# Gated linear attention: gate projection ahead of the values, Silu applied later in place

## The chip, the cores and the metric

The kernel runs on one core of one Trainium2 chip. The metric is the device time of one execution in microseconds (us). Three runs of the kernel before took 2588.95, 2592.64 and 2594.71 us, so the median is 2592.64 us. One further execution was profiled; all rows below come from it.

## The reference

A two-layer decoder trunk over 1024 tokens of width 1024, in float32. Layer 0 mixes tokens by differential attention, layer 1 by gated linear attention (GLA); each is followed by a gated MLP with a short convolution. The change touches only GLA, which has 4 heads with keys of 128 and values of 256:

```
q, k, v, r = split(h @ w_in)                      # per head: 128, 128, 256, 256 columns
g = log_sigmoid((h @ w_a1) @ w_a2 + b_a) / 16
b = cumsum(g) inside a chunk
attn[i,j] = sum_d q[i,d] k[j,d] exp(b[i,d] - b[j,d]),  j <= i
o = (q exp(b)) @ state + attn @ v
state = exp(b_last) state + (k exp(b_last - b))^T @ v
out = (rms_norm(o) * silu(r)) @ w_o
```

## The kernel before

Every large product is made from a high and a low part of each operand (hi*hi, hi*lo, lo*hi), so a weight block of 128x1024 is loaded by DMA into a staging buffer `st` (three of them), its high part is cast on ScalarE (line 122, `wh`) and its low part is taken on GpSimd (line 123, `wl`). There are two `wh` and two `wl` buffers. `load_w` hands out blocks in the order of the list `order` and has the next one split ahead as far as a buffer is free.

A head's projections are cut into units. `qk_units` has 4 (queries and keys, two token halves each), `r_units` 4 (the output gate r, two halves of 128 columns by two token halves), `v_units` 8 (values, one for each block of 128 tokens). A q, k or r unit is 24 matmuls with 512 columns and ends in one 128x512 eviction from PSUM; a v unit is 24 matmuls with 256 columns and ends in a ScalarE cast and a VectorE subtraction. A v unit needs both of the head's value blocks, so v holds both weight buffers until its last unit; q, k and r need one block for two units. Units are closures; `run(units, n)` takes the next n of a list at the place in the program where it stands. A scheduler then fixes one instruction order for each engine, in which work that is not ready gives way to later work that is; on the chip each engine runs its order as it stands.

One head goes through these stages in the loop over `hd`:

- `decay(hd)`: b from the gate's low-rank input `z1`: a matmul `psg`, Abs, Exp and Ln on ScalarE, a GpSimd subtraction, eight scans on VectorE.
- levels: attention inside chunks of 128 is built from a diagonal and 7 levels. `prepare(m)` makes one scaled operand `d` (two VectorE subtractions, one ScalarE Exp, one GpSimd product with k, one VectorE product with q), `put` multiplies it with itself on TensorE into `psl` (two PSUM buffers) and copies the valid part into `acc` on VectorE (lines 996 and 998). `d` comes from a ring of four buffers.
- `across`, `inside`, `cross`, `key_T`: q and k scaled for use across chunks, `acc` split into parts, the products between neighbouring chunks (`psx`), the transposed keys (`psk`).
- `state`: three steps of the running state (`pss`); `outputs` and `finish`, for two token halves (`og`): output, norm, product with silu(r) (line 1087), and later (`rest`, lines 274 to 286 and 1097) the scale by the norm, written to DRAM (for the last head, kept in SBUF).

Before, the 8 value units of a head begin at the end of the head before it (2 units) and go on in its levels; the 4 r units stand at `inside`, `cross` and `state`, and are evicted by Silu straight from PSUM (line 913). After the last of them an instruction (line 916) loads ScalarE's table with Exp and Ln back. The 4 q and k units of the next head follow at `state` and `outputs`. After the last head the list ends with the units of the output projection (`first_units`, tile `pacc`).

Of the kernel before, what the change touches and what calls it, by code (L numbers as in the profile page):

```python
# [13 lines left out]
AF = mybir.ActivationFunctionType  # L14
# [7 lines left out]
NT = T // P  # L22
# [24 lines left out]
def trunk(ctx, tc, x, norm_mix, norm_ffn, norm_final, wqk, wv, w_o, lam_in, subln,  # L47
          gqk, gv, gr, ga1, ga2, gba, gnorm, g_o, wup, conv, wdn,
          cos_t, sin_t, causal, lvl_mask, ident_in, out):
    nc = tc.nc  # L50
# [27 lines left out]
    def slot(i, name, dt=F32, shape=None):  # L78

        return slots.tile(shape or [P, 1024], dt, name=name, tag=f"s{i}")  # L80
# [23 lines left out]
    order, loaded = [], []  # L104
# [56 lines left out]
    def half(hf):  # L161
        return slice(512 * hf, 512 * hf + 512)
# [684 lines left out]
    def gla(proj):  # L847
# [18 lines left out]
        q, k, b, vs, sr, fac = {}, {}, {}, {}, {}, {}  # L866
# [21 lines left out]
        def qk_units(hd):  # L888
            q[hd], k[hd] = slot(2 * (hd % 2), "q"), slot(2 * (hd % 2) + 1, "k")
            W = {}  # L890

            def unit(s, hf):
                if hf == 0:
                    W[s] = load_w(gqk[2 * hd + s])
                ps = mm_ps("psq")
                project_T(ps, W[s], hf)
                if s == 0:
                    nc.scalar.mul(q[hd][:, half(hf)], ps, DK ** -0.5)
                else:
                    nc.scalar.copy(k[hd][:, half(hf)], ps)  # L900
                flush()
            return [lambda s=s, hf=hf: unit(s, hf) for s in range(2) for hf in range(2)]

        def r_units(hd):
            sr[hd] = [slot(6 + e, "r") for e in range(2)]
            W = {}

            def unit(e, hf):
                if hf == 0:
                    W[e] = load_w(gr[2 * hd + e])  # L910
                ps = mm_ps("psr")
                project_T(ps, W[e], hf)
                last = nc.scalar.activation(sr[hd][e][:, half(hf)], ps, AF.Silu)
                if e == 1 and hf == 1:
                    with tc.issue_after(getattr(last, "ins", last)):
                        nc.scalar.preload_act_table_set("natural_log_exp_and_others")
            return [lambda e=e, hf=hf: unit(e, hf) for e in range(2) for hf in range(2)]

        def v_units(hd):
            vs[hd] = [[slot(14 + 2 * i + hf, "v" + "hl"[i], F32R, [P, 4, DV]) for hf in range(2)] for i in range(2)]  # L920
            W = []

            def unit(t):
                if t == 0:
                    W.extend(load_w(gv[2 * hd + i]) for i in range(2))
                ps = mm_ps("psv")
                project_tok(ps[:, :DV], W, t)
                vh, vl = (z[t // 4][:, t % 4, :] for z in vs[hd])
                nc.scalar.copy(vh, ps[:, :DV])
                nc.vector.tensor_tensor(vl, ps[:, :DV], f32(vh), op=ALU.subtract)  # L930
            return [lambda t=t: unit(t) for t in range(NT)]
# [70 lines left out]
        def across(hd):  # L1002

            bv = b[hd].rearrange("p (c w) -> p c w", c=NCH)
            tot = bv[:, :, CH - 1:CH]
            fac[hd] = small.tile([P, NCH, 1], F32, name="fac", tag="fac", bufs=2)
            nc.scalar.activation(fac[hd], tot, AF.Exp, scale=1.0 / 16)
            kd, qd = d_ring("kd"), d_ring("qd")
            kv = kd.rearrange("p (c w) -> p c w", c=NCH)
            nc.vector.tensor_tensor(kv, tot.broadcast_to([P, NCH, CH]), bv, op=ALU.subtract)  # L1010
            nc.scalar.activation(kd, kd, AF.Exp, scale=1.0 / 16)
            nc.scalar.activation(qd, b[hd], AF.Exp, scale=1.0 / 16)
            nc.gpsimd.tensor_tensor(k[hd], kd, k[hd], op=ALU.mult)
            nc.vector.tensor_tensor(q[hd], qd, q[hd], op=ALU.mult)


        def inside(hd, av):
            EH, EL = (slot(18 + i, "e" + "hl"[i], F32R, [P, 4, 2, P]) for i in range(2))
            O = slot(20, "odd", F32R, [P, 2, 4, P])
            for src, hi, lo in ((av[:, 0::2, :], EH[:, :, 0, :], EL[:, :, 0, :]),  # L1020
                                (av[:, 1::2, :], O[:, 0], O[:, 1])):
                nc.scalar.copy(hi, src)
                nc.gpsimd.tensor_tensor(lo, src, f32(hi), op=ALU.subtract)
            return EH, EL, O

        def cross(hd, A):
            EH, EL, _ = A
            ps = mm_ps("psx")
# [74 lines left out]
        def run(units, n=1):  # L1103
            for _ in range(n):
                if units:
                    units.pop(0)()
# [1 line left out]
        for u in qk_units(0):  # L1108
            u()
        nc.scalar.preload_act_table_set("natural_log_exp_and_others")  # L1110
        nxt = v_units(0)
        gates()
        run(nxt, 2)
        decay(0)
        for hd in range(GH):
            vu = nxt
            av, diagonal, prepare, put = level_units(hd)
            diagonal()
            ds = []
            for n, m in enumerate(LEVELS):  # L1120
                ds.append(prepare(m))
                if n >= 1:
                    put(n - 1, ds[n - 1])
                run(vu)
            put(len(LEVELS) - 1, ds[-1])
            run(vu, NT)
            last = hd == GH - 1
            nxt = r_units(hd) + (proj.first_units() if last else qk_units(hd + 1))
            across(hd)
            A = inside(hd, av)  # L1130
            run(nxt)
            cross(hd, A)
            run(nxt)
            kT = key_T(hd)
            S = slot(21, "S", F32, [P, 3, DV])
            for B in range(3):
                if B < 2:
                    run(nxt)
                state(hd, B, kT, S)
            if not last:  # L1140
                decay(hd + 1)
            run(nxt, 2)
            rest = finish(hd, 0, outputs(hd, 0, A, S))
            run(nxt, 2)
            rest()
            rest = finish(hd, 1, outputs(hd, 1, A, S))
            run(nxt, 1)
            if not last:
                nxt = v_units(hd + 1)
                run(nxt, 2)  # L1150
            else:
                run(nxt, 3)
            rest()
            if last:
                run(nxt, NT)
# [4 lines left out]
    for layer, w_out in enumerate((w_o, g_o)):  # L1160
        order += [w_out[k] for k in ((0, 1, 2, 3, 6, 7), (0, 1, 4, 6, 7))[layer]] + [None]
        if layer == 0:
            order += [gqk[0], gqk[1]]
            for hd in range(GH):
                order += [gv[2 * hd], gv[2 * hd + 1]]
                order += [gr[2 * hd], gr[2 * hd + 1]]
                order += [gqk[2 * hd + 2], gqk[2 * hd + 3]] if hd + 1 < GH else []

    st = {}
# [27 lines left out]
    proj = OutProjection(0, w_o, 0, lambda t: x[t * P:(t + 1) * P, :])  # L1197
# [109 lines left out]
```

## Time and profile before

| | |
|---|---|
| runs | 2588.95, 2592.64, 2594.71 us |
| profiled execution | 2591.02 us, of it 2589.2 us span |
| granted TensorE clock, mean | 0.98 |
| TensorE busy | 2472.1 us (95%) |
| VectorE, ScalarE, GpSimd busy | 63%, 40%, 46% |

The span is the time from the first to the last instruction of the program in the trace; 1.8 us lie around it. PE is TensorE, DVE VectorE, ACT ScalarE, POOL GpSimd, SP the queue that issues DMAs. Rows give the start of an instruction in us from the span's start, its duration, its engine and line, and in brackets how long the engine had been idle before it and what ended that. Matmuls overlap, so the duration of one is longer than the distance to the next. GLA lies between about 1344 and 1800 us of the span.

### The profile page before, as it was taken

To read this page: it belongs to the slowest core of one execution; us is meant where nothing else is said; L and a number is where in the kernel's file an instruction comes from. 1 tells how busy PE (TensorE), PEld (TensorE's weight loads), DVE (VectorE), ACT (ScalarE), POOL (GpSimd) and SP (SyncE) were. 2 spreads that over 40 slices of the span, in tenths; PEclk is the share of its full clock that TensorE was granted. 3 is DMA by queue.
4 is the path that set the end of the run, shared out by engine and by line. 5 is a ranking of instruction groups with operands and counts; after the bars stand their busy time and mean duration, and the time that the engine had idled before them with its cause. 6 is when DMAs were issued, how large, how long until landed. Compare 5 with 4: busy or idle time off the path is not lost. (4 is left out here: it accounts for less than half of the span.)

```text
span 2589.2 us, 30822 instructions
## 1 busy us (share of the span) xinstructions
PE 2472.1 (95%) x11752; PEld 2012.3 (78%) x11752; DVE 1627.7 (63%) x2218; ACT 1032.8 (40%) x1630; POOL 1202.9 (46%) x723
## 2 busy tenths in 40 slices
PE   7999999988999999999998999998889999999998
PEld 5777777776788888788887888787768888887887
DVE  5577777876666666644456467386566666665445
ACT  4454454534454454421133334332245445442111
POOL 3444445325555555554414344353355555554441
PEclk9999999999999999999999999999989999999999
DMA  5222222433122222443221111123312222234331
GB/s 175 64 63 58 58 58 57 126 122 127 63 89 81 75 82 85 176 132 98 93 83 33 50 33 33 50 95 129 110 66 81 88 76 82 84 126 156 114 98 65
DMA packets 66020, 228.61 MB, mean 88 GB/s; under 512 B 8144, under 2 KB 8784, under 8 KB 65872
## 3 DMA queue, kind: packets, MB, share of 16 engines
q1 hardware_dynamic: 65872, 226.64, 26.6%
q8 instruction: 92, 1.51, 0.3%
q14 instruction: 56, 0.46, 0.1%
HBM read 163.17 MB, written 50.86 MB: 83 GB/s over the span
## 5 line engine op out<-in xcount | busy, mean ns | idle before, releaser
L308 DVE TENSOR_TENSOR res<-pacc,res 128x512 f32<-128x512 f32 x408 | 280.0, 690 | 273.4 <-PE pacc L144 272.8
L478 POOL TENSOR_TENSOR uw<-st,uw 128x512 fp32r<-128x512 f32 x190 | 287.9, 1515 | 238.1 <-ACT uw L477 228.4
L123 POOL TENSOR_TENSOR wl<-st,wh 128x1024 fp32r<-128x1024 f32 x55 | 141.5, 2577 | 264.7 <-ACT wh L122 264.7
L142 PE MATMUL pacc<-wdh,gh 128*128 128x512 f32 x512 | 200.7, 394 | 5.9 <-DVE res L308 5.9
L143 PE MATMUL pacc<-wdl,gh 128*128 128x512 f32 x512 | 202.5, 395 | 0.1
L144 PE MATMUL pacc<-wdh,gl 128*128 128x512 f32 x512 | 201.9, 394 | 0.0
L557 DVE SCALAR_TENSOR_TENSOR b<-cu,cv,b 128x1023 f32<-128x1023 f32 x44 | 62.3, 1416 | 186.7 <-ACT b L556 186.7
L477 ACT CAST uw<-st 128x512 fp32r<-128x512 f32 x190 | 118.1, 621 | 110.7 <-PE ps_z L144 55.6
L142 PE MATMUL psq<-XH,wh 128*128 128x512 f32 x384 | 157.2, 410 | 1.2 <-DVE ms L172 0.7
L604 POOL TENSOR_TENSOR gl<-st,gh 128x1024 fp32r<-128x1024 f32 x32 | 78.1, 2439 | 165.1 <-ACT gh L603 122.4
L143 PE MATMUL psq<-XL,wh 128*128 128x512 f32 x384 | 154.2, 401 | 0.5 <-DVE ms L172 0.4
L144 PE MATMUL psq<-XH,wl 128*128 128x512 f32 x384 | 153.1, 399 | 0.0
L753 ACT ACTIVATE p<-p,nmax 128x256 f32<-128x256 f32 (+7 forms) x128 | 99.0, 776 | 86.1 <-DVE nmax L750 84.9
L122 ACT CAST wh<-st 128x1024 fp32r<-128x1024 f32 x59 | 61.6, 1047 | 161.0 <-PE pacc L144 53.3
L142 PE MATMUL pacc<-wh,gh 128*128 128x512 f32 x256 | 107.0, 421 | 19.6 <-DVE XL L239 10.9
L603 ACT CAST gh<-st 128x1024 fp32r<-128x1024 f32 x32 | 33.6, 1049 | 215.5 <-PE pacc L143 157.7
L478 POOL TENSOR_TENSOR wh<-st,wh 128x512 fp32r<-128x512 f32 x56 | 85.6, 1529 | 70.9 <-ACT wh L477 70.9
L142 PEld LDWEIGHTS pacc<-wdh,gh 128*128 128x128 f32 x512 | 96.9, 189 | 27.8 <-DVE res L308 6.7
L478 POOL TENSOR_TENSOR wl<-st,wl 128x512 fp32r<-128x512 f32 x56 | 84.5, 1509 | 66.8 <-ACT wl L477 64.7
L143 PEld LDWEIGHTS pacc<-wdl,gh 128*128 128x128 f32 x512 | 96.9, 189 | 22.9 <-POOL wdl L604 1.0
L144 PEld LDWEIGHTS pacc<-wdh,gl 128*128 128x128 f32 x512 | 96.9, 189 | 21.1
L750 DVE CUSTOM_DVE_ANT_0 p<-s_ps,mask 128x256 f32<-128x256 f32 (+7 forms) x128 | 91.5, 750 | 26.7 <-PE pta L773 22.7
(356 smaller groups left out, 7429.7 us busy)
## 6 DMA issues: line engine op xcount, KB each, us to landing
st<-in_wup_dram SPq DMA_DIRECT2D x88, 512.0 KB, 3.5
g_scr<-a SPq DMA_DIRECT2D x44, 512.0 KB, 2.6
st<-in_wdn_dram SPq DMA_DIRECT2D x44, 512.0 KB, 3.6
st<-g_scr SPq DMA_DIRECT2D x44, 512.0 KB, 3.3
r_scr<-res SPq DMA_DIRECT2D x24, 512.0 KB, 3.2
res<-r_scr SPq DMA_DIRECT2D x24, 512.0 KB, 5.6
st<-in_wqk_dram SPq DMA_DIRECT2D x16, 512.0 KB, 3.5
st<-o_scr SPq DMA_DIRECT2D x13, 512.0 KB, 3.4
```

What stands on the lines that cost most here:

```text
L122: nc.scalar.copy(hi, st)
L123: (eng_lo or nc.gpsimd).tensor_tensor(lo, st, f32(hi), op=ALU.subtract)
L142: nc.tensor.matmul(ps, lhsT=ah, rhs=bh, start=first, stop=False, **kw)
L143: nc.tensor.matmul(ps, lhsT=ah, rhs=bl, start=False, stop=False, **kw)
L144: nc.tensor.matmul(ps, lhsT=al, rhs=bh, start=False, stop=last, **kw)
L308: nc.vector.tensor_tensor(res[t][:, half(dh)], ps, res[t][:, half(dh)], op=ALU.add)
L477: nc.scalar.copy(w[:, half(0)], src)
L478: nc.gpsimd.tensor_tensor(w[:, half(1)], src, f32(w[:, half(0)]), op=ALU.subtract)
L557: nc.vector.scalar_tensor_tensor(u[:, 1:], c[:, :T - 1], cv[:, n, 1:2], u[:, 1:], op0=ALU.mult, op1=ALU.add)
L604: nc.gpsimd.tensor_tensor(lo, st, f32(hi), op=ALU.subtract)
L750: nc.vector.tensor_tensor_reduce(out=pm[:, :w], in0=s_ps[:, :w], in1=st["mask"][:, T - w:], scale=-0.125, scalar=3.0e38, op0=ALU.add, op1= ...
L753: nc.scalar.activation(pm[:, :w], pm[:, :w], AF.Exp, bias=nmax, scale=-1.0, accum_out=sums[:, m:m + 1])
```

## The change

The four r units go ahead of the eight v units in one list. The list is begun at the end of the head before, after `outputs` (2 units; in head 0 after `gates`), goes on in the levels (7 units) and ends at `inside`, `cross` and `key_T` (one unit each). The q and k units of the next head then have a list of their own and begin in `state`. The weight order is changed to match. The r units are evicted by a plain copy; `silu` then applies Silu in place, 128x1024 twice, and is put behind the last Exp of `across` on ScalarE, with the table load behind it. Heads take turns in two pairs of r buffers (slots 26, 27 and 6, 7), since r of the next head is made while the last one's is in use.

```diff
         def r_units(hd):
-            sr[hd] = [slot(6 + e, "r") for e in range(2)]
+            sr[hd] = [slot((26 if hd % 2 == 0 else 6) + e, "r") for e in range(2)]
...
-                last = nc.scalar.activation(sr[hd][e][:, half(hf)], ps, AF.Silu)
-                if e == 1 and hf == 1:
-                    with tc.issue_after(getattr(last, "ins", last)):
-                        nc.scalar.preload_act_table_set("natural_log_exp_and_others")
+                nc.scalar.copy(sr[hd][e][:, half(hf)], ps)
...
+        def silu(hd, behind):
+
+            with tc.issue_after(behind):
+                for e in range(2):
+                    last = nc.scalar.activation(sr[hd][e], sr[hd][e], AF.Silu)
+            with tc.issue_after(last.ins):
+                nc.scalar.preload_act_table_set("natural_log_exp_and_others")
...
-            nc.scalar.activation(qd, b[hd], AF.Exp, scale=1.0 / 16)
+            last = nc.scalar.activation(qd, b[hd], AF.Exp, scale=1.0 / 16)
...
+            return last.ins
...
-        nxt = v_units(0)
+        nxt = r_units(0) + v_units(0)
...
-            vu = nxt
...
-                run(vu)
+                run(nxt)
             put(len(LEVELS) - 1, ds[-1])
-            run(vu, NT)
             last = hd == GH - 1
-            nxt = r_units(hd) + (proj.first_units() if last else qk_units(hd + 1))
-            across(hd)
+            behind = across(hd)
             A = inside(hd, av)
+            silu(hd, behind)
             run(nxt)
             cross(hd, A)
             run(nxt)
             kT = key_T(hd)
+            run(nxt)
+            qk = [] if last else qk_units(hd + 1)
             S = slot(21, "S", F32, [P, 3, DV])
             for B in range(3):
                 if B < 2:
-                    run(nxt)
+                    run(qk)
                 state(hd, B, kT, S)
-            if not last:
+            if last:
+                nxt = proj.first_units()
+                run(nxt, 2)
+            else:
                 decay(hd + 1)
-            run(nxt, 2)
+                run(qk)
+                nxt = r_units(hd + 1) + v_units(hd + 1)
             rest = finish(hd, 0, outputs(hd, 0, A, S))
-            run(nxt, 2)
+            run(qk or nxt, 1 if qk else 2)
             rest()
             rest = finish(hd, 1, outputs(hd, 1, A, S))
-            run(nxt, 1)
-            if not last:
-                nxt = v_units(hd + 1)
-                run(nxt, 2)
-            else:
-                run(nxt, 3)
+            run(nxt, 4 if last else 2)
             rest()
...
             for hd in range(GH):
+                order += [gr[2 * hd], gr[2 * hd + 1]]
                 order += [gv[2 * hd], gv[2 * hd + 1]]
-                order += [gr[2 * hd], gr[2 * hd + 1]]
                 order += [gqk[2 * hd + 2], gqk[2 * hd + 3]] if hd + 1 < GH else []
```

## Rows read from the trace of the kernel before

**Rows 1.** The page's busy times of the engines (share of the span, instructions), and the TensorE clock granted in 40 equal slices of the span, in tenths.

```profile
PE 2472.1 (95%) x11752; PEld 2012.3 (78%) x11752; DVE 1627.7 (63%) x2218; ACT 1032.8 (40%) x1630; POOL 1202.9 (46%) x723
...
PEclk9999999999999999999999999999989999999999
```

**Rows 2.** Windows from the first value unit of one head to that of the next (heads 0, 1 and 2): length, busy time of each engine with instructions, clock granted, DMA share and GB/s.

```profile
1376.74:1478.23 101.49, 95.69 (x600) 84.97 (x598) 55.73 (x83) 42.81 (x57) 49.07 (x21) 0.98 0.11 32
1478.23:1581.58 103.35, 96.88 (x600) 86.08 (x599) 63.58 (x81) 36.23 (x50) 44.90 (x21) 0.97 0.13 41
1581.58:1684.51 102.93, 96.46 (x601) 85.73 (x599) 63.55 (x81) 36.23 (x50) 44.90 (x21) 0.97 0.13 42
```

**Rows 3.** What TensorE waited for between 1343 and 1756 us: us in all, times, the longest.

```profile
PE psl L994 <- DVE acc L998: 15.5, 3, 5.2
...
PE psl L994 <- POOL d L983: 2.6, 1, 2.6
...
PE psl L994 <- DVE r L1087: 1.7, 3, 0.6
PE psl L994 <- DVE d L984: 1.6, 2, 1.1
PE psr L144 <- POOL wl L123: 0.6, 1, 0.6
```

**Rows 4.** TensorE at the end of head 1's levels, in order of time.

```profile
1512.48 1.95 PE L994 MATMUL psl<-d 128*128 128x128 f32 x16
1514.19 0.48 PE L142 MATMUL psr<-XH,wh 128*128 128x512 f32 x1
...
1520.06 3.75 PE L994 MATMUL psl<-d 128*128 128x128 f32 x16 [5.16 <-DVE acc L998]
```

**Rows 5.** Windows around that wait, and one of head 0; columns as in rows 2 (before the clock: PE, PEld, DVE, ACT, POOL).

```profile
1514.90:1520.00 5.10, 0.00 (x1) 0.00 (x0) 5.10 (x5) 0.14 (x1) 5.10 (x3) 0.88 0.34 113
1520.00:1525.00 5.00, 4.94 (x23) 4.97 (x24) 4.36 (x4) 0.00 (x0) 0.53 (x1) 0.50 0.61 199
...
1413.50:1421.00 7.50, 6.86 (x32) 6.09 (x33) 5.25 (x6) 2.60 (x3) 7.50 (x3) 0.81 0.22 70
```

**Rows 6.** VectorE and then GpSimd over the same wait, in order of time, and the durations of line 1097 from 1478 to 1590 us (minimum, median, maximum, ns; first and last start).

```profile
1512.71 5.60 DVE L1097 TENSOR_TENSOR r<-r,sq 128x512 f32<-128x512 f32 x2
...
1518.58 1.34 DVE L998 COPY_PREDICATED acc<-masks,psl 128x1024 f32<-128x1024 int32 x1
...
1504.31 7.93 POOL L983 TENSOR_TENSOR d<-d,k 128x512 f32<-128x512 f32 x2 [6.97 <-ACT d L982]
1512.31 2.71 POOL L1013 TENSOR_TENSOR k<-kd,k 128x1024 f32<-128x1024 f32 x1
1514.97 5.56 POOL L123 TENSOR_TENSOR wl<-st,wh 128x1024 fp32r<-128x1024 f32 x2
1525.91 1.30 POOL L1023 TENSOR_TENSOR el<-acc,eh 128x512 fp32r<-128x512 f32 x1 [5.37 <-ACT eh L1022]
...
L1097 DVE TENSOR_TENSOR r<-r,sq x6: 684/692/2858, 1482.0 to 1586.0; 128x512 f32<-128x512 f32 x6
```

**Rows 7.** Windows of one kind of instruction alone, busy time of TensorE first: two q units, two v units, and all of `psl`, `pss` and `og` in one head.

```profile
1553.24:1564.47 11.23, 11.23 (x48) 8.85 (x47) 0.00 (x0) 0.60 (x1) 1.00 0.16 48
...
1478.23:1484.17 5.94, 5.94 (x48) 5.87 (x48) 0.00 (x0) 0.00 (x0) 1.00 0.31 119
...
1581.58:1684.51 102.93, 15.32 (x116) 13.91 (x116) 9.40 (x8) 0.97 0.13 42
...
1581.58:1684.51 102.93, 2.59 (x18) 2.43 (x18) 1.39 (x3) 0.97 0.13 42
...
1581.58:1684.51 102.93, 8.87 (x62) 8.09 (x60) 2.81 (x4) 2.05 (x2) 0.97 0.13 42
```

**Rows 8.** ScalarE in order of time: the eviction of head 1's last key unit, the last Exp of `across`, the table load ahead of the r evictions, a weight block's cast, the last r eviction with the second table load, and `decay`.

```profile
1474.39 0.58 ACT L900 COPY k<-psq 128x512 f32<-128x512 f32 x1
...
1511.85 1.04 ACT L1012 ACTIVATE qd<-b 128x1024 f32<-128x1024 f32 x1
...
1526.37 1.28 ACT L913 ACT_TABLE_LOAD   x1
...
1549.09 1.05 ACT L122 CAST wh<-st 128x1024 fp32r<-128x1024 f32 x1 [5.79 <-PE psr L143]
1550.04 0.59 ACT L913 ACTIVATE r<-psr 128x512 f32<-128x512 f32 x1
1550.65 1.28 ACT L916 ACT_TABLE_LOAD   x1
1551.95 0.69 ACT L940 ACTIVATE e<-psg,ba 128x512 f32<-128x512 f32 x1
```

**Rows 9.** Head 0: the first matmul of `decay` on TensorE, the scans that end `decay` on VectorE. The last head: what TensorE waited for from 1756 to 1850 us.

```profile
1379.62 0.39 PE L939 MATMUL psg<-z,a 128*128 128x512 f32 x1
...
1389.64 2.63 DVE L946 TENSOR_TENSOR_SCAN b<-ones_f,e 128x128 f32<-128x128 f32 x8 [1.78 <-POOL e L944]
...
PE pacc L142 <- ACT gh L128: 4.5, 1, 4.5
PE pacc L142 <- DVE res L308: 4.1, 2, 3.5
```

**Rows 10.** What the DMA queue (SP) waited for between 1340 and 1810 us: us in all, times, the longest.

```profile
SPq L1101 <- DVE r L1097: 111.0, 9, 31.9
```

## The prediction

> **What bounds the kernel now.** I read the page first. TensorE is busy for 95% of the span at nearly full clock, and no other engine is above 63% [rows 1]; so the end is set by TensorE's work and by the time it stands idle, and a change that removes no matmul can win only idle time and slow-clock time. Next, windows one head long. Heads 1 and 2 take 103.35 and 102.93 us, with the clock at 0.97 [rows 2]. Third, TensorE's waits: in GLA the largest is `psl` (a level's matmuls) waiting for `acc`, 15.5 us in three waits of at most 5.2, one in each of heads 1 to 3 [rows 3]. Fourth, the order around it: after the sixth level TensorE has two r matmuls, and then idles for 5.16 us before the seventh [rows 4]. The seventh needs the PSUM buffer that line 998 frees, and VectorE does this only at 1518.58, behind two products of line 1097 that took 5.60 us for both, while GpSimd was busy without a break from 1512.31 to 1520.5; alone such a product takes 0.69 [rows 6]. The r matmuls could not fill the hole: their weights come into the buffers that v has just left, and the `wl` of both blocks ran from 1514.97 to 1520.53 [rows 6]. Last, the windows behind the wait: TensorE is granted 0.50 for the next 5 us, its lower level of 1.2 GHz, after 5.1 us of idling [rows 5], and a level that takes 1.95 us takes 3.75 [rows 4].
>
> So in a head there is one stage where VectorE and GpSimd end last. From the end of the eviction of the head's last key unit (1474.97, rows 8) to the seventh level (1520.06, rows 4) pass 45.1 us. TensorE has there, from [rows 7]: eight v units at 2.97 (23.8), half of `og` (4.4), and the diagonal with six levels (15.3 less the slow 3.75: 11.6). That is 39.8, which is 5.3 short, the wait seen. In the rest of the head the other engines wait for TensorE.
>
> **The change, part by part.**
>
> *More matmuls beside the levels.* The stretch from the last key to the seventh level now holds four r units (5.6 each by a q unit of the same shape, 22.5) and five v units (14.9) with the same 16.0: 53.4 us [rows 7] against 45.1 that the other engines need. The wait of 5.2 is covered with 8.3 to spare. Three v units are left for the stage behind (8.9 against 22.5 of r). Gone in heads 1 to 3: 15.5 us of waiting [rows 3], and with it the slow clock: 5 us at 0.50 did 2.5 us of work [rows 5], so 3 x 2.5 = 7.5. Bounds: 0 if the wait stays (a rival below), 23.0 if both go. I take 23.0.
>
> *Head 0.* It has waits of 2.6 and 1.6 (for `d`) and 0.6 [rows 3], 4.8, and 7.5 us at a clock of 0.81 [rows 5], 7.5 x 0.19 = 1.4: 6.2 at most. But `decay(0)` now stands behind two r units, 11.2 us, where before its first matmul came at 1379.62, 2.9 us after the first v matmul [rows 2, 9]. Its scans end at 1392.27 [rows 9] and would end some 8 us later. The levels begin later, beside fillers that are longer by 13.6 (37.4 against 23.8). I take half of the gain, 3.1; bounds 0 and 6.2.
>
> *Weights, r to v.* Within the levels v needs both weight buffers, and r's second is free only after its last unit. A cast is 1.05 [rows 8] and a `wl` 2.8 with VectorE working [rows 6], 3.8 together; half a v unit (1.5) and a level (1.7, a seventh of 11.6) lie between. 0.6 is left, as much as the one wait of an r unit for `wl` [rows 3]. Bounds 0 and 2.3 (no level ready). Four heads at 0.6: 2.4 lost.
>
> *Weights, v to q.* This is the hand-over that v to r was before. Behind the last v unit TensorE has `pss` (2.6, rows 7) to do while 3.8 go by, and the first buffer is free 1.5 before the end, as v reads its first block in its first half; so between 0 and 1.2. If GpSimd still has `el` and `odd` ahead (2 x 1.3, rows 6), 3.8. I take 0.6 for each head (in the last one the output projection's blocks take the place of q's), 2.4 lost.
>
> *Silu.* Four evictions at 0.59 become four copies at 0.58 (as for k) and two in-place passes over 128x1024, 1.04 each by the Exp of that size: 2.1 us more of ScalarE a head, which is busy 36 of 103 us [rows 2, 8]. The two table loads stay two, but move from both ends of the r units to right behind the last Exp of `across`; there ScalarE is held for 1.28 + 2.1 + 1.28 = 4.7 us, while v units of 2.97 wait for their cast. With four PSUM buffers two units fit into it, so I cost it at nothing; if other tiles hold two of the buffers, 4.7 less one or two units is a wait of up to 1.7 a head. The casts of `acc` come after the seventh level, later still. One load no longer stands directly ahead of `decay` (1550.65, rows 8); nothing waits for that, so it is worth nothing either.
> The rows show a load of 1.28 with the next instruction 0.02 behind it [rows 8]. The Trainium skill (ScalarE: Activation LUTs, What ACT_TABLE_LOAD costs) gives a drain with each load, about 2.66 us a switch. By that the stretch would be 7.4 and could cost 1.5 us a head, 6 in all, a forecast of 2577; the trace disagrees on the drain, and I go by its 1.28.
>
> *Queues and buffers.* No DMA is added; weight loads change places only. SP holds a weight load behind the store of the last head's output, which waits for line 1097, up to 31.9 us [rows 10]. Three staging buffers keep loads ahead of the splits, as now; if a block came late its price is a wait like those above. The second r pair costs SBUF alone.
>
> Sum: -23.0 - 3.1 + 2.4 + 2.4 = -21.3. The profiled execution took 2591.02 (span 2589.2 and 1.8 around it), so 2569.7 there. It lies 1.6 under the median of the runs shown; against that, 2592.6 - 21.3 = 2571.3, say **2571**.
>
> **The rivals.**
>
> *The wait stays, since order and not supply makes it (chance 0.18).* TensorE runs a fixed order. If the fillers are put ahead of the sixth level, the seventh still stands next in line while VectorE is held up. For: the 5.60 us for line 1097 come from GpSimd's work beside it, and an order that expects 0.69 each sees no reason to put more there. Against: the longer fillers push every level later, whatever stands between the last two. One v unit in place of two r matmuls (2.97 for 0.9) would leave 3.1 of 5.2; gain 3 x 2.1, the slow clock partly, head 0's 3.1, less 4.8: some 5 us, 2588.
> The Trainium skill (SBUF — State Buffer, Who interferes with whom) says that a VectorE instruction with both inputs in SBUF and a GpSimd one that reads SBUF exclude each other for a whole instruction. The trace agrees (0.69 to 2.8). By it each split that lands among the levels can hold VectorE for its length.
>
> *Slower: v to q becomes the hole (0.12).* Place: TensorE behind the last v unit, where q's first block must pass GpSimd. For: a GpSimd product of levels in line ahead can take up to half of 7.93 for two, and beside it `el` and `odd` take 2.6 [rows 6]; the r units that covered this stage are gone. Against: ScalarE and GpSimd were idle there (5.37 before `el`, rows 6). It decides from 6.5 us a head: (23.0 + 3.1) / 4. At 6.5 of waiting and 2.5 of slow clock, 9 a head, the time is 2591.0 + 36 - 26 and 1.6 more: 2603.
>
> *The last head gives part of it back (0.10).* It has no next q and k, so three v units alone cover `cross`, `key_T` and `state`, where 22.5 of r did. The tail then waits as it does now, 4.5 and 4.1 [rows 9], and some 6 to 8 more: 2578.
>
> **How the numbers follow.** Forecast 0.60 (with its costs, 2561 to 2582), the last head 0.10, wait stays 0.18, slower 0.12. The least is a gain of 31: 23.0, 6.2 and 1.7 of small waits. With the slow case partly out and the 0.18 in, the range is 2561 to 2594. A measurement of this kernel can tell 0.2%, 5.2 us. Faster takes the forecast, the last head and part of the third case: 0.76; same 0.12; slower 0.12.
>
> **What would show it.** Right: `psl` waiting for `acc` gone or under 1 us in heads 1 to 3, no window of 5 us at 0.50 behind it, heads 1 and 2 at 95 to 98 us each, four r copies and two 1.04 us passes in a head, still two table loads. Wrong in the weights: q or v units waiting for `wl` L123 over 2 us a head. Wrong in Silu: v units waiting for PSUM that ScalarE frees. Wrong altogether if the fillers leave the levels' stretch or a head keeps 103 us.

## The result and the profile after

Four runs of the changed kernel took 2558.16 to 2561.3 us, median 2559.2, beside four of the kernel before on the same chip at 2588.95 to 2594.71, median 2590.9. The ratio is 0.9877, with an interval of 0.986 to 0.9894: 31.7 us faster. The profiled execution took 2561.3 us with a span of 2559.5, 29.7 less than the span before. The forecast of 2571 had the right sign, and the time lies 2 us below the low end of its range. The profiled execution is the slowest of the four, so its terms add up to 29.7 and not to 31.7.

Busy times of the kernel after, to be read against [rows 1]:

```profile
PE 2463.2 (96%) x11752; PEld 2005.7 (78%) x11752; DVE 1618.4 (63%) x2218; ACT 1040.7 (41%) x1638; POOL 1187.5 (46%) x723
```

The matmuls are as many as before. TensorE's busy time fell by 8.9 us all the same, which is clock and not work. Next the windows, first those of the kernel after: from 1343 us, about where GLA begins, to head 0's first r unit, then from each head's first r unit to the next one's, the last one up to the long run of the output projection (columns as in [rows 2]).

```profile
1343.00:1373.32 30.32, 28.47 (x130) 22.63 (x128) 7.26 (x16) 6.78 (x11) 5.19 (x2) 1.00 0.21 69
...
1373.32:1474.61 101.29, 96.10 (x600) 86.17 (x598) 54.18 (x81) 43.76 (x57) 45.67 (x20) 0.97 0.10 32
1474.61:1568.85 94.24, 94.04 (x601) 83.59 (x599) 60.17 (x80) 38.20 (x52) 41.21 (x21) 1.00 0.14 45
1568.85:1663.27 94.42, 94.09 (x601) 83.64 (x599) 60.29 (x80) 38.20 (x52) 40.99 (x21) 1.00 0.14 46
1663.27:1773.63 110.36, 100.86 (x624) 87.83 (x622) 89.19 (x104) 45.23 (x60) 47.55 (x24) 0.99 0.32 110
```

Two windows of the kernel before that [rows 2] does not have, the stretch ahead of head 0 and the last head:

```profile
1343.00:1376.74 33.74, 29.75 (x124) 23.56 (x123) 8.68 (x15) 6.78 (x11) 4.73 (x2) 0.90 0.17 51
...
1684.51:1803.35 118.84, 103.81 (x624) 90.59 (x622) 88.60 (x102) 41.75 (x56) 52.03 (x23) 0.95 0.29 102
```

The five differences are -3.4, -0.2, -9.1, -8.5 and -8.5, together -29.7: all of the span's gain lies here. Length less TensorE's busy time is its idling. In head 1 that fell from 6.47 to 0.20, in head 2 from 6.47 to 0.33, in head 3 from 15.03 to 9.50: 17.9 us. Busy time in the same three heads fell by 8.2 us (2.8, 2.4 and 3.0) as the clock rose from 0.97, 0.97 and 0.95 to 1.00, 1.00 and 0.99. That is 26.1 of the 29.7. The 94.2 and 94.4 of heads 1 and 2 lie under the 95 to 98 forecast.

What TensorE waited for in the kernel after, from 1343 to 1730 us (us in all, times, the longest), against [rows 3]:

```profile
PE psl L999 <- DVE d L989: 5.2, 1, 5.2
PE psz L881 <- DVE wh L877: 1.4, 1, 1.4
PE psv L142 <- DVE el L1040: 1.2, 1, 1.2
PE psv L143 <- POOL wl L123: 0.9, 3, 0.3
```

The three waits for `acc` are gone. One of 5.2 us is new, in head 0. In the last head, behind this window, the waits for `res` fell from 4.1 to 2.5. The end of head 1's levels, against [rows 4, 6]: TensorE's seventh level, VectorE's two products of line 1103 (1097 before), the copy of line 1003 (998 before) that frees a PSUM buffer and the instruction ahead of it, and ScalarE over Silu.

```profile
1523.42 1.95 PE L999 MATMUL psl<-d 128*128 128x128 f32 x16
...
1500.94 1.30 DVE L1103 TENSOR_TENSOR r<-r,sq 128x512 f32<-128x512 f32 x2
1516.31 0.42 DVE L935 TENSOR_TENSOR vl<-psv,vh 128x256 fp32r<-128x256 f32 x1 [1.44 <-ACT vh L934]
1516.65 1.37 DVE L1003 COPY_PREDICATED acc<-masks,psl 128x1024 f32<-128x1024 int32 x1
...
1472.12 0.58 ACT L900 COPY k<-psq 128x512 f32<-128x512 f32 x1
...
1517.26 1.28 ACT L920 ACT_TABLE_LOAD   x1
1518.55 2.00 ACT L920 ACTIVATE r<-r 128x1024 f32<-128x1024 f32 x2
1520.57 1.28 ACT L922 ACT_TABLE_LOAD   x1
1521.87 0.37 ACT L934 CAST vh<-psv 128x256 fp32r<-128x256 f32 x1
```

The seventh level runs without a wait and at full clock, 1.95 us where it took 3.75. The last key eviction ends at 1472.70 and the buffer is free at 1518.02, 45.3 us later (45.0 before). TensorE comes to the level at 1523.42, 50.7 us after that eviction, where it came too early before. VectorE is not pressed any more: the two products took 1.30 us where they took 5.60, it idled for 1.44 us just ahead of the copy, and the copy empties a level that TensorE began only at 1514.10. So 45.3 is not what the other engines need, and its closeness to 45.0 is chance.

### The profile page after: what moved, and what is told of

It is laid out like the page before. It is cut to its first block, busy times and chain, and to the rows that moved or that the text cites. A ratio compares the mean times of both kernels' runs of the same rounds, so it can differ in the third digit from the quotient of the medians.

```text
span 2559.5 us, 30819 instructions
## 1 busy us (share of the span) xinstructions
PE 2463.2 (96%) x11752; PEld 2005.7 (78%) x11752; DVE 1618.4 (63%) x2218; ACT 1040.7 (41%) x1638; POOL 1187.5 (46%) x723
```

## The experiments

**Theory A, the prediction's:** the waits end because more matmuls stand beside the levels, and r's matmuls could not stand there before for want of their weights. **Rival B:** the supply of matmuls is the same in every head; what decides is where the fixed order of TensorE puts the seventh level against VectorE's chain, which GpSimd holds up. **Rival C:** Silu in place, and fewer table loads in the way, is what gained.

**Is it Silu?** Into the kernel before, copies at the eviction and Silu in place, with the order of units left as it was:

```diff
-                last = nc.scalar.activation(sr[hd][e][:, half(hf)], ps, AF.Silu)
...
+                nc.scalar.copy(sr[hd][e][:, half(hf)], ps)
...
                 state(hd, B, kT, S)
+            silu(hd, behind)
```

> The kernel before with only the eviction changed: r units end in a plain copy, Silu is applied in place, two passes over 128x1024, behind state and ahead of decay. If Silu's form has no part in the gain, the time stays within 0.2% of the kernel before (2586 to 2596), and TensorE's wait for acc at the end of the levels stays at 5.2 us in heads 1 to 3. Rival: the evictions by Silu and their table loads held TensorE back; then 5 us or more are won here.

2586.15 us, ratio 0.999 (0.9977 to 1.0004); the three waits for `acc` still sum to 15.4. The other way round, the changed kernel with Silu back at the eviction:

```diff
-                nc.scalar.copy(sr[hd][e][:, half(hf)], ps)
+                last = nc.scalar.activation(sr[hd][e][:, half(hf)], ps, AF.Silu)
+                if e == 1 and hf == 1:
+                    with tc.issue_after(getattr(last, "ins", last)):
+                        nc.scalar.preload_act_table_set("natural_log_exp_and_others")
...
-            silu(hd, behind)
```

> The changed kernel with Silu back at the eviction of each r unit, and the table load behind the last of them. The r units now lie among the Exps of the norm and the levels, so ScalarE must change tables back and forth: up to two loads of 1.28 us for each of the four units, 5 to 10 us a head on ScalarE in place of 2.6. Supply theory: TensorE has some 5 us to spare at the seventh level, so most of it is hidden: 0 to 4 us a head, 2559 to 2575. Rival (the in-place form is what carries the change): the waits for the levels come back and the time is that of the kernel before or above.

2569.36 us, ratio 0.9929 (0.9905 to 0.9954): 9 to 13 us over the changed kernel, by the medians of the changed kernel's two sets of runs or by the ratios to the kernel before. ScalarE's table loads in one head (1474 to 1570 us; busy, mean ns, and idle before), and what TensorE then waited for (1343 to 1730):

```profile
L913 ACT ACT_TABLE_LOAD x4 | 5.1, 1283 | 0.1
L990 ACT ACT_TABLE_LOAD x3 | 3.8, 1283 | 4.7 <-DVE d L989 4.7
...
PE ssp L280 <- DVE hl L271: 4.7, 3, 1.6
PE psv L143 <- POOL wl L123: 2.1, 2, 1.1
```

Each r eviction now falls between two Exps of the levels and loads twice; with three more loads there are ten a head in place of two. So Silu in place wins nothing alone, and 9 us or more once r stands in the levels; without it 18.9 us of the gain are left. C falls as the source of the gain.

**Is it the order of units?** The changed kernel with v ahead of r again in the combined list:

```diff
-        nxt = r_units(0) + v_units(0)
+        nxt = v_units(0) + r_units(0)
...
-            silu(hd, behind)
             run(nxt)
...
             run(nxt)
+            silu(hd, behind)
...
-                nxt = r_units(hd + 1) + v_units(hd + 1)
+                nxt = v_units(hd + 1) + r_units(hd + 1)
...
-                order += [gr[2 * hd], gr[2 * hd + 1]]
                 order += [gv[2 * hd], gv[2 * hd + 1]]
+                order += [gr[2 * hd], gr[2 * hd + 1]]
```

> The changed kernel with the two lists swapped: eight v units, then four r units, taken at the same places of the program, Silu in place behind the last r unit. TensorE then has, from the last key eviction to the seventh level, eight v units and one r unit: 23.8 + 5.6 + 16.0 = 45.4 us, just what the other engines need there (45.1). Supply theory (the wait goes when TensorE has more work beside the levels than the other engines need): the wait of 5.2 shrinks to 0 to 2 us, but the weights' hand-over from v to r lies at the end of the levels as in the kernel before, so 2 to 5 us of it may remain: 2566 to 2585. Rival (the list's place alone matters, the r units being made beside the levels at all, with a double pair of r buffers): within 4 us of the changed kernel, 2555 to 2563.

2591.36 us over ten runs, ratio 1.0016 (1.0003 to 1.003): the whole gain is lost, which neither side expected. TensorE's largest waits from 1343 to 1730 us:

```profile
PE psl L999 <- DVE r L1093: 9.8, 3, 4.0
PE ssp L279 <- DVE hl L270: 9.6, 3, 3.5
```

The waits of 5 us for `acc` are gone here too, yet 19.4 us of idling stand at the start of the levels, where before had 3.7. What covers one end uncovers the other. So the gain hangs on the order: r first has both ends covered at once.

Half of it, two r units ahead of v and two behind:

```diff
+            return r[:2] + v_units(hd) + r[2:]
...
-            silu(hd, behind)
...
+            silu(hd, behind)
...
-                order += [gr[2 * hd], gr[2 * hd + 1]]
-                order += [gv[2 * hd], gv[2 * hd + 1]]
+                order += [gr[2 * hd], gv[2 * hd], gv[2 * hd + 1], gr[2 * hd + 1]]
```

> The changed kernel with the list in another order: two r units, eight v units, two r units (Silu in place behind the last). From the last key eviction to the seventh level TensorE then has two r and seven v units: 11.2 + 20.8 + 16.0 = 48.0 us of work that has its weights, against 45 to 47 that the other engines need, where the changed kernel has 53 and the list with v first had some 41 (its r unit could not start). Supply theory: waits of 0 to 2 us a head, 2559 to 2570. Rival (all four r units must be ahead, or the order of the weights decides): the time of the list with v first, 2585 or more.

2578.96 us, ratio 0.9967 (0.995 to 0.9983), between what the two sides expected. The waits for `acc` are gone; new ones stand behind the levels (1343 to 1850 us), here in head 1 with TensorE in order of time:

```profile
PE psk L1051 <- DVE k L1044: 6.8, 4, 2.1
PE psk L1051 <- DVE vl L935: 3.4, 3, 1.1
...
1530.90 0.40 PE L143 MATMUL psr<-XL,wh 128*128 128x512 f32 x1
1533.40 0.66 PE L1051 MATMUL psk<-ident,k 128*128 128x128 f32 x4 [2.10 <-DVE k L1044]
...
1535.61 0.48 PE L144 MATMUL psr<-XH,wl 128*128 128x512 f32 x1
```

Two r matmuls run, and then the transposes of `key_T` stand next in line, too early for VectorE; the other r matmuls come behind them. It is the picture of [rows 4] at another place. In the changed kernel v units run there with one wait of 1.2 us in three heads, so the three that it keeps for `inside`, `cross` and `key_T` are part of the gain.

**Was it r's weights?** In the kernel before, the first r block gets buffers of its own and is split at the start of the levels:

```diff
-                    W[e] = load_w(gr[2 * hd + e])
+                    W[e] = load_w(gr[2 * hd + e]) if e else early.pop()
...
             diagonal()
+            early.append(split(staged(gr[2 * hd]), 26, 27, "gr"))
...
-                order += [gr[2 * hd], gr[2 * hd + 1]]
+                order += [gr[2 * hd + 1]]
```

> The kernel before, order and Silu as they were, with one edit: the first r weight block of a head is split into two free buffers of its own (slots 26 and 27) at the start of the levels, so two r units (11.2 us) have their weights when v ends. Supply theory: TensorE then has work with its weights in the hole before the seventh level, 39.8 + 11.2 = 51 us against 45; the wait for acc of 5.2 us in heads 1 to 3 goes to 0 to 1.5 us, the lower clock behind it goes too, and the time falls by 15 to 24 us, to 2566 to 2575, without r ahead of v. Rival (only r ahead of v gives it, as the order of TensorE is fixed and the r matmuls would be put behind the seventh level anyway): within 5 us of the kernel before.

2588.25 us over ten runs, ratio 0.9997 (0.9986 to 1.0009). GpSimd's split, and TensorE in order of time:

```profile
1467.05 2.39 POOL L129 TENSOR_TENSOR grl<-st,grh 128x1024 fp32r<-128x1024 f32 x1 [2.92 <-ACT grh L128]
...
1512.48 0.48 PE L142 MATMUL psr<-XH,grh 128*128 128x512 f32 x1
1512.80 0.40 PE L143 MATMUL psr<-XL,grh 128*128 128x512 f32 x1
1518.35 3.75 PE L995 MATMUL psl<-d 128*128 128x128 f32 x16 [5.15 <-DVE acc L999]
1521.76 0.77 PE L144 MATMUL psr<-XH,grl 128*128 128x512 f32 x1
```

The weights lie ready 43 us ahead, two r matmuls go as before, and TensorE idles for 5.15 us at the seventh level with the third r matmul next in line. The order holds it, not the weights.

So the two r units were put ahead of the seventh level by hand, in heads 0 to 2, with the early block:

```diff
+            if not last:
+                run(nxt, 2)
             put(len(LEVELS) - 1, ds[-1])
             run(vu, NT)
```

> The kernel before with the first r weight block split early into its own buffers, as in the run where the wait stayed, and one more edit: in heads 0 to 2 the two r units of that block stand ahead of the seventh level in the program. Order theory (TensorE runs a fixed order; work whose weights are there is of use only where it stands ahead of the waiting matmuls): in heads 1 and 2 the wait of 5.2 us for acc goes to 0 to 0.5, and each of these heads falls from 103 to 94 to 97 us, while head 3, left as it was, keeps its wait of 5.2; in all 10 to 20 us less than the kernel before, 2569 to 2579. Rival (the wait has another cause that r's weights and place don't touch): heads 1 and 2 keep 102 to 104 us.

2611.97 us, ratio 1.0094 (1.0065 to 1.0122): slower by some 20 us, and no theory had that. The seventh level of head 1, the start of the next head's levels, and the waits of head 2:

```profile
1539.95 0.40 PE L144 MATMUL psr<-XH,grl 128*128 128x512 f32 x1
1540.19 1.95 PE L995 MATMUL psl<-d 128*128 128x128 f32 x16
...
1482.96 0.50 PE L969 MATMUL psl<-ph,ones 128*128 128x512 f32 x1 [3.34 <-ACT ph L965]
...
PE psl L995 <- DVE acc L999: 8.0, 3, 4.1
PE psl L969 <- ACT ph L965: 3.3, 1, 3.3
```

At its place the edit does what B says: no wait, full clock. The new waits lie at the start of the next head's levels: the diagonal waits 3.3 us for `ph`, the next v units come behind it, and the first levels wait for VectorE, in heads 1 to 3. That the two units taken from the end of the head before are what is missing there is argued from the two experiments on the order of units, not shown. Why the scheduler then leaves the v units out of the first levels was not followed up.

**The other cure.** If VectorE's chain sets the seventh level, shortening it must do as well. In the kernel before, the second half's `rest` (with line 1097) is owed until the next head's levels are through:

```diff
+            if owed:
+                owed.pop()()
...
-            rest()
             if last:
+                rest()
...
+            else:
+                owed.append(rest)
```

> The kernel before with one edit: the scale by the norm of a head's second half (lines 274 to 286 and 1097, of it the two products that took 2.8 us each beside GpSimd) is issued behind the next head's levels, so VectorE is free of it in the levels. If VectorE's and GpSimd's 45 us set the seventh level, the stretch gets 5 to 8 us shorter there, the wait for acc falls from 5.2 to 0 to 2 us a head, and the time falls by 8 to 23 us, to 2567 to 2582. Rival: the weight splits of r at that place hold VectorE just as long at another instruction; then the wait stays over 3 us.

2572.25 us, ratio 0.9945 (0.993 to 0.996). Its heads 1 and 2, and its largest wait behind the one for `psz` (1343 to 1730):

```profile
1480.34:1574.56 94.22, 93.97 (x600) 83.78 (x599) 59.74 (x81) 36.22 (x50) 42.84 (x21) 1.00 0.13 45
1574.56:1668.70 94.14, 92.56 (x591) 82.46 (x589) 59.93 (x80) 36.22 (x50) 40.92 (x20) 1.00 0.14 45
...
PE psr L144 <- POOL wl L123: 3.4, 3, 1.4
```

The wait for `acc` is gone and these heads are as fast as with the change, with v ahead of r and Silu at the eviction. So TensorE may come later, or VectorE earlier: B's mechanism shown from both sides. The rest of the change's gain is not had this way: the last head, up to the end of TensorE's wait for `gh`, takes 116.4 us (1668.70 to 1785.06) where the changed kernel takes 110.4. The change has something of both, a later TensorE and shorter products on VectorE; no run separates the two.

**What do the hand-overs of weights cost?** In the changed kernel the `wl` of the q and k blocks of heads 1 to 3 was taken twice (an instruction repeated, the result the same):

```diff
-        (eng_lo or nc.gpsimd).tensor_tensor(lo, st, f32(hi), op=ALU.subtract)
+        for _ in range(2 if any(str(src) == str(z) for z in [gqk[i] for i in range(2, 2 * GH)]) else 1):
+            (eng_lo or nc.gpsimd).tensor_tensor(lo, st, f32(hi), op=ALU.subtract)
```

> The changed kernel with one cost doubled: the low part of each q and k weight block of heads 1 to 3 is taken twice on GpSimd, 2.4 us more for each of six blocks. The prediction gave the hand-over from v to q 0.6 us a head with TensorE's cover nearly used up; then this adds 2 to 3 us a head for the first block, 6 to 9 in all. Rival: the cover has several us to spare (state, the first part of the outputs); then the time stays within 2 us of the changed kernel and TensorE's wait for wl of q stays under 0.5 a head.

2565.54 us, ratio 0.9909 (0.9894 to 0.9923), 5 us over the changed kernel run beside it, between the two sides. No q unit waits for `wl`; the waits are at r to v:

```profile
PE psv L143 <- ACT wh L122: 3.5, 3, 1.2
PE psv L144 <- POOL wl L124: 3.3, 3, 1.1
```

The instruction order changed with the edit: TensorE has more `og` matmuls ahead of the rest of q than in the changed kernel. So part of the room is made by the order.

The same with the value blocks, by `[gv[i] for i in range(2 * GH)]` in that line:

> The changed kernel with the low part of each value block taken twice on GpSimd, 2.4 us more for each of eight blocks. The hand-over from r to v had 0.3 us of waiting a head in the changed kernel. If its cover is used up, TensorE waits 2 to 3 us a head more for wl of v, 8 to 12 us in all. Rival: a level's matmuls fill in and less than 1 us a head is seen.

2570.69 us in the one run, which gives no interval, with waits of `psv` of 3.8 us for `wl` and 1.5 for `wh`, three each, and of 7.0 for head 0's `d`. So v to q takes 2.4 us more in heads 1 to 3 without a wait of q. The 4.8 us that the doubled value blocks add to r to v in each head show as 1.8 of waiting (5.3 in three), between the two sides, so about 3 are covered there.

**Head 0 and its 5.2 us.** `decay(0)` ahead of the two r units:

```diff
-        run(nxt, 2)
         decay(0)
+        run(nxt, 2)
```

> The changed kernel with one edit: head 0's decay stands ahead of the first two r units in the program. In the changed kernel TensorE idles 5.2 us in head 0 before its first level and runs the two levels behind it at the lower clock (4.75 us for 32 matmuls that take about 3.5 elsewhere). If that hole is there because decay came behind 11.2 us of r matmuls, the decay matmuls now come as soon as z1 is written, some 8 us earlier, the scans end near 1389 us of the span instead of 1397, the hole falls under 1 us and the time is 4 to 7 us below the changed kernel (about 2553). Rival: the hole stays because head 0's first levels are bound by GpSimd and VectorE taking turns on the first four operands (VectorE 1400 to 1406 us there); then under 2 us is won.

2560.36 us, ratio 0.9889 (0.9862 to 0.9916): as the changed kernel. The scans end 8 us earlier, at 1389.2, and the wait for `d` goes from 5.2 only to 3.4, while a `psg` wait of 1.0 and a `psz` wait of 3.5 us stand beside it. The changed kernel was then run again beside the next ones:

> The changed kernel once more, beside the next three on one chip. In its profile the wait of TensorE for the gate's first weights in head 0 (psz for line 877) was 1.4 us, in the five other profiles at hand (the kernel before and four variants) it is 3.5, with the same program up to there. If the 1.4 was chance (VectorE and GpSimd starting 0.06 us apart and one of them waiting for the other), this execution shows 3.5 and a span some 4 us longer from there; if it belongs to the changed kernel, it shows 1.4 again. The time: 2556 to 2564.

2560.35 us, ratio 0.9886 (0.9871 to 0.9901). Its `psz` wait is 3.5 us, so the 1.4 above was chance; the run with the early r block, another kernel, had 1.4 as well. VectorE's and GpSimd's instructions that start together there, in the first profile of the changed kernel and then in this one:

```profile
1364.72 0.89 DVE L877 TENSOR_TENSOR wh<-st,wh 128x128 fp32r<-128x128 f32 x4
1365.06 2.80 POOL L968 TENSOR_TENSOR pr<-k,q 128x1024 f32<-128x1024 f32 x1 [3.66 <-ACT k L900]
```

```profile
1363.84 3.03 DVE L877 TENSOR_TENSOR wh<-st,wh 128x128 fp32r<-128x128 f32 x4
1364.18 2.34 POOL L968 TENSOR_TENSOR pr<-k,q 128x1024 f32<-128x1024 f32 x1 [3.65 <-ACT k L900]
```

The starts are 0.34 us apart in both, not 0.06; in one case GpSimd's instruction is stretched by 0.46 us, in the other VectorE's by 2.1. To take away what makes VectorE late, `a1` got a slot of its own in place of a weight buffer, beside `decay(0)` ahead:

```diff
-            a1 = wpool.tile([P, 1024], F32R, name="wh", tag="wh", bufs=2).rearrange("p (k c) -> p k c", k=KT)
+            a1 = slot(13, "a1", F32R).rearrange("p (k c) -> p k c", k=KT)
```

> The changed kernel with decay ahead of the first r units in head 0, and the gate's first weights in a buffer of their own, so that they don't wait for the last key unit to leave a weight buffer. If the 3.5 us wait of psz comes from that buffer alone, it goes, and with it the lower clock behind it (psz takes 10.1 us there against 7.7): 5 to 6 us less than the changed kernel where that shows 3.5, and 2 us more by decay: 2550 to 2556. Rival: the wait is only moved to the next thing that comes late in head 0 (the operands of its first levels), and the time stays within 2 us of the changed kernel.

2554.57 us, ratio 0.9866 (0.9849 to 0.9882), all four runs (2551.56 to 2556.19) below all of the changed kernel beside them (2559.93 to 2560.86). The `psz` wait is gone and the 32 matmuls of `psz` run at full clock:

```profile
1361.14:1368.60 7.46, 7.46 (x32) 5.82 (x31) 1.38 (x2) 0.59 (x1) 1.00 0.22 75
```

This beats both kernels. The buffer without `decay(0)` ahead was not run; `decay(0)` ahead alone won nothing. Against the last 3.4 us for `d`, head 0's later subtractions were put behind the first level's product with q:

```diff
+                with tc.issue_after(first[0]) if hd == 0 and first else nullcontext():
```

> The kernel with decay ahead and the gate's weights in their own buffer, with one more edit, in head 0 alone: the VectorE subtractions of the second and later levels are put behind the first level's product with q. There TensorE still waits 3.4 us for the first level's operand, while VectorE makes the subtractions of four levels in turn with GpSimd. If that order makes the hole, the first operand is ready some 7 us earlier, the hole goes with the lower clock behind it, and the time falls by 3 to 5 us, to 2549 to 2552. Rival: the hole moves to the second or third level, whose operands now come later; then the time stays within 2 us of 2554.6.

2553.95 us, ratio 0.9867 (0.9851 to 0.9884), the same: the wait for `d` is gone and a `psv` wait of 2.6 us for `wh` stands in its place.

## Why the prediction was right or wrong

**The wait and the slow clock (-23.0): right in cause and nearly in size.** The forecast was 15.5 of waiting and 7.5 of clock; the waits for `acc` are gone, and heads 1 to 3 lost 8.2 of busy time. TensorE's supply of 53.4 came out at 50.7, mostly because the half of `og` counted as 4.4 took 1.9 (1472.70 to 1474.61). The 45.1 us were taken for a fixed need of the other engines, and they are not: with r first the products of line 1103 fell from 5.60 to 1.30 us, and VectorE waits at that place. The room of 8.3 us is 5.4 (1518.02 to 1523.42). An estimate from these rows: with the old 5.60 the copy would come some 2.6 us later (4.3 less VectorE's idling of 1.44 and 0.25 ahead of it), and 2.8 would be left; so the later TensorE would do, and the lighter VectorE, which the sum did not foresee, adds to it.

**Small waits, left standing in the sum: wrong.** [rows 3] has 1.7 us of `psl` waiting for `r`; the kernel before has 2.0 of `ssp` waiting for `hl` besides. They stand between the diagonal and the first levels, and r units, with weights in place, cover them too. With 15.5, 3.7 and 1.6 of the 4.1 for `res` gone, 0.9 and 1.2 new, named waits make 18.7; idling for which the profile names nothing grew by 0.8, so 17.9 in all.

**The hand-overs of weights (+4.8): the step that failed.** They cost 0.9 at r to v and nothing at v to q, where 2.4 were put on each. In head 1, the second v block's low part, the v matmul that waits for it, the first matmul behind the last v unit, and q's first:

```profile
1503.35 2.83 POOL L123 TENSOR_TENSOR wl<-st,wh 128x1024 fp32r<-128x1024 f32 x1
1506.23 0.38 PE L143 MATMUL psv<-wl,XH 128*128 128x256 f32 x1 [0.20 <-POOL wl L123]
...
1535.61 0.28 PE L143 MATMUL og<-el,vh 128*128 128x256 f32 x1
1537.39 0.45 PE L142 MATMUL psq<-XH,wh 128*128 128x512 f32 x1
```

At r to v both sides of the difference were too small. From the last r unit's end (1500.42) to the low part (1506.18) pass 5.8 us and not 3.8, since cast and split stand behind an Exp and a product of the levels; TensorE has two levels and 22 v matmuls there, where one level and half a unit were counted. 0.3 a head is left where 0.6 was put, and some 3 us more could be covered. The row of 0.6 that the difference was held against is a wait at another place of the order, with another cover. At v to q only `pss` was counted; 1.8 us of `og` matmuls stand ahead of q as well.

**Head 0 (-3.1): wrong, -0.2.** The later scans cost as feared: they end at 1397.2, where they ended at 1392.27 [rows 9], and one hole of 5.2 us replaces the small ones. With `decay(0)` ahead the scans come early and 3.4 remain, so they are not all of it.

**Ahead of head 0 (nothing): -3.4.** The `psz` wait is shorter by 2.1, which is chance, and the `psz` matmuls by some 2 us, at the higher clock (below); the last part of a microsecond or so the other way was not followed up. The two terms hold as a sum better than one by one: with the long `psz` wait, the second profile of the changed kernel has 31.60 us up to head 0 and 100.27 in it, 131.87 together, where the first has 131.61 and the kernel before 135.23. How much of the clock's part belongs to the change is open.

The sum of -21.3 became -29.7 in the profiles. Of the 8.4 between them, the hand-overs make 3.9, the small waits 3.7, the stretch ahead of head 0 3.4, `res` 1.6 and the clock 0.7; against them stand head 0 with 2.9, the new wait for `el` with 1.2 and the unnamed idling with 0.8. The low end of the range, a gain of 31, had all 6.2 of head 0 in it, which did not come, and nothing for the stretch ahead of it; that 29.7 lies so near is luck.

**Silu (nothing): right.** Its 1.28, 2.00 and 1.28 hold ScalarE for 4.6 us and no TensorE wait follows. The next instruction starts 0.02 us behind the second load, so the drain that the Trainium skill adds (ScalarE: Activation LUTs, What ACT_TABLE_LOAD costs) is not seen here either, and the 6 us by it did not come.

**The reason given for the hole: wrong.** "The r matmuls could not fill the hole: their weights come into the buffers that v has just left" is refuted by the early block: the wait stayed, 5.15 us. The rival that named the order had the right mechanism, and the wrong outcome for this change, because the change alters that order: more fillers stand ahead of every level.

**The rivals.** v to q did not become the hole: doubling its split left no q unit waiting. The last head gave nothing back, at -8.5 us like the others; its three v units suffice.

## What to carry to other kernels

A wait of the busiest engine is to be read with the instruction that stands behind it: work that could run fills nothing while the fixed order has another matmul ahead of it, and it may be cured by making the busiest engine later or the other one earlier. Where moved units cover a stage, list all stages that the same units must cover, in their order; in three experiments moving units from one end went with new waits at another. Take the need of the other engines as a result of the order too, not as a fixed number. Small waits in the same stage go with the large one and belong in the sum, and a hand-over's price holds only with the cover of the place where it was measured.

## What the hardware showed

Two instructions on VectorE and GpSimd that start 0.34 us apart take turns, and which one waits varies between executions: the same four subtractions took 0.89 or 3.03 us, and TensorE then waited 1.4 or 3.5. The Trainium skill (SBUF — State Buffer, Who interferes with whom) has the exclusion of the two, and the rows agree.

The same idle time does not always cost clock. Behind a wait of 3.54 us each, the 16 `psz` matmuls of line 882 (nanoseconds: minimum, median, maximum; first and last start) in the kernel before and in the second profile of the changed kernel:

```profile
L882 PE MATMUL psz<-XL,wh x16: 392/399/628, 1367.4 to 1376.5; 128*128 128x512 f32 x16
```

```profile
L882 PE MATMUL psz<-XL,wh x16: 392/397/400, 1367.3 to 1374.4; 128*128 128x512 f32 x16
```

From first to last they take 9.1 us in the one and 7.1 in the other; the granted clock was 0.74 from 1366.80 to 1376.90 in the one and 1.00 from 1367.00 to 1374.60 in the other. With the same wait, the long form is also in the profiles with `decay(0)` ahead, with v ahead of r, with half of r ahead, with Silu in place alone and with the norm later, and nearly as long (8.5) with two r units ahead of the seventh level; the short one is in those with Silu at the eviction and with either split doubled. What sets it was not found.
